# Rotary embedding in float32 on one core: 1 MB of x loaded first, larger end pieces, and five tiles instead of four added on TensorE

## The chip, the cores and the metric

The kernel runs on one core of a Trainium2 chip. Times are device microseconds (us) of one execution. A kernel is run several times; one run of the kernel before took 231.49 us instead of 164.6. It counts as slow and enters no ratio. A ratio here is the mean time of one kernel's fast runs over the mean of the other's fast runs in the same rounds, so it is not quite the ratio of the medians that are quoted beside it.

## The reference

x has shape (8, 2048, 8, 64): batch, position, head, feature. cos and sin have shape (2048, 32). Everything is float32.

```python
x1, x2 = x[..., :32], x[..., 32:]
out1 = x1 * cos - x2 * sin
out2 = x1 * sin + x2 * cos
return np.concatenate([out1, out2], axis=-1)
```

About 33.5 MB are read and 33.5 MB written, so the question is how close the kernel comes to keeping the DMA engines full.

## The kernel before

x is cut into 16 slabs of 2 MB (128 partitions x 4096 columns, 16 KB a partition). Nine slab buffers (`xt`) are used in turn. A slab is worked on in two units of 2048 columns, and its result is written over x in the same buffer. A unit is of one of three kinds:

```python
    kinds = {}
    for i in (5, 10):
        kinds |= {(i, 0): "C", (i, UNIT): "B"}
    # A: GpSimd t2 = x_swapped*(-sin, sin); VectorE t1 = x*cos; VectorE xt = t1 + t2
    # B: GpSimd t2, VectorE t1 as in A; TensorE adds them (eye @ t1 + eye @ t2 in PSUM);
    #    ScalarE copies the sum from PSUM to xt, 512 columns at a time
    # C: VectorE t1 = x*cos and t2 = x*sin, no GpSimd; TensorE adds with eye and -eye; ScalarE copies
```

So B takes one VectorE pass away, and C takes GpSimd's two multiplies away; both give ScalarE four copies. The loads are issued by SyncE, the stores by ScalarE:

```python
    def cuts(i):                      # loads of slab i, in columns
        if i == 0:
            return [HD, HD, 2 * HD, UNIT]     # HD = 512, UNIT = 2048
        return [SLAB]                          # 4096
    def pieces(i):                    # units of work of slab i
        if i == 0:
            return [HD, HD, 2 * HD, UNIT]
        if i == last:
            return [UNIT, 2 * HD, HD, HD]
        return [UNIT, UNIT]
    # ... load(0) issues sin after its first cut; cos is loaded on ScalarE's queue
    LAG = 2
    for i in range(last + 1):
        if i == last:
            for k in range(i - LAG, i):
                store(k, 0, SLAB)
        for lo, n in spans(pieces(i)):
            rotate(i, lo, n)                   # B and C put copies on ScalarE here
            if i == last:
                store(i, lo, n)
        if LAG <= i < last:
            store(i - LAG, 0, SLAB)            # issued by ScalarE, behind those copies
        if i > LAG and i - LAG - 1 + NBUF <= last:
            load(i - LAG - 1 + NBUF)           # needs the store of slab i - 3
```

The copies and the stores are kept in program order on ScalarE. When slab 5 has copies, the stores of slabs 3 and 4 stand behind all eight of them.

## Time and profile before

| | before |
|---|---|
| time, median | 164.64 us (runs: 164.57, 164.64, 231.49) |
| span of the profiled run | 163.0 us |
| DMA | 67.66 MB, mean 415 GB/s, both queues together 98% of sixteen engines' span |
| VectorE, GpSimd busy | 143.4 us (88%), 139.4 us (86%) |

From the page of the kernel before: the busy tenths of VectorE, GpSimd and the DMA engines in 40 slices of 4.1 us, and the two DMA queues (q1 has the loads that SyncE issues, q10 the stores and cos that ScalarE issues).

```profile
DVE  0587999999999999999899999999999999999900
POOL 1599999999999999799999999956999999995000
DMA  4999999999999999999999999999999999999995
...
q1 hardware_dynamic: 2880, 33.82, 49.5%
q10 hardware_dynamic: 2880, 33.82, 48.7%
```

The DMA line has no slice below 9 between the first and the last. VectorE and GpSimd are nearly as full, but they finish 8 and 12 us before the span does. So the bytes bound this kernel, and the other engines matter where they leave the DMA engines without work.

The Trainium skill, page "DMA: Bandwidth & Descriptors", section "Specifications", gives a fabric ceiling of 435 GB/s. The trace agrees: 431 GB/s on average between 30 and 150 us, and 424 to 439 in its stretches of 10 us (the views count a packet whole where it starts, so a stretch can come out a little above the ceiling).

The next lines are from the timeline of the kernel before. Columns: start, duration, engine, line, operation, output and inputs, count; in brackets the idle time before it and what ended it. They show where VectorE starts slab 10's C unit and when ScalarE is done with that slab's copies.

```profile
100.21 2.28 DVE L144 TENSOR_TENSOR t<-xt,cos_ps 128x2048 f32<-128x2048 f32 x1
...
119.32 0.59 ACT L158 COPY xt<-o 128x512 f32<-128x512 f32 x1 [1.13 <-PE o L157]
119.38 3.26 ACTq L183 DMA_DIRECT2D out_dram<-xt  x4
```

Between the C unit's start and the batch of stores lie 19.2 us (19.3 us for slab 5: 55.53 to 74.83). In that time no store is issued, though slabs 8 and 9 are finished, and the DMA engines live on loads. Such a stretch is called a hold below: hold 1 belongs to the first slab with a C unit, hold 2 to the second. The individual DMA packets in the trace show how close the loads came to running out. This table was worked out from those packets, not printed by the profile; "first packet" is when the first of the sixteen engines starts on it, "landed" is when the first and the last engine is done.

```
kernel before            issued   first packet   landed (first, last engine)
load  of slab 11          52.15      72.99         77.79 - 79.25   last load queued in hold 1
store of slab 3           74.83      77.80         82.68 - 83.91   first held store
load  of slab 15         109.91     116.75        121.60 - 123.43  last load of all
store of slab 8          119.38     121.61        126.47 - 127.68  first held store
```

Each time the held stores arrived shortly before the loads ended.

### The profile page before, as it was taken

To read this page: it belongs to the slowest core of one execution; us is meant where nothing else is said; L and a number is where in the kernel's file an instruction comes from. 1 tells how busy PE (TensorE), PEld (TensorE's weight loads), DVE (VectorE), ACT (ScalarE), POOL (GpSimd) and SP (SyncE) were. 2 spreads that over 40 slices of the span, in tenths; PEclk is the share of its full clock that TensorE was granted. 3 is DMA by queue.
4 is the path that set the end of the run, shared out by engine and by line. 5 is a ranking of instruction groups with operands and counts; after the bars stand their busy time and mean duration, and the time that the engine had idled before them with its cause. 6 is when DMAs were issued, how large, how long until landed. Compare 5 with 4: busy or idle time off the path is not lost. (4 is left out here: it accounts for less than half of the span.)

```text
span 163.0 us, 480 instructions
## 1 busy us (share of the span) xinstructions
PE 33.3 (20%) x64; PEld 13.4 (8%) x64; DVE 143.4 (88%) x71; ACT 12.0 (7%) x20; POOL 139.4 (86%) x74
## 2 busy tenths in 40 slices
PE   0000000000000079993000000899920000000000
PEld 0000000000000024440000000244400000000000
DVE  0587999999999999999899999999999999999900
ACT  3300000000000002232000000022410000000000
POOL 1599999999999999799999999956999999995000
PEclk9999999999999999999555555579997555555555
DMA  4999999999999999999999999999999999999995
GB/s 137 383 432 442 406 398 426 438 438 418 438 434 426 430 434 430 426 434 438 422 428 438 424 422 446 430 414 446 434 422 430 442 422 422 446 426 430 434 402 207
DMA packets 5763, 67.66 MB, mean 415 GB/s; under 512 B 640, under 2 KB 640, under 8 KB 1664
## 3 DMA queue, kind: packets, MB, share of 16 engines
q1 hardware_dynamic: 2880, 33.82, 49.5%
q10 hardware_dynamic: 2880, 33.82, 48.7%
q14 instruction: 3, 0.02, 0.0%
HBM read 34.08 MB, written 33.55 MB: 415 GB/s over the span
## 5 line engine op out<-in xcount | busy, mean ns | idle before, releaser
L138 POOL TENSOR_TENSOR t<-xt,sin_sb 128x1024 f32<-128x1024 f32 (+2 forms) x34 | 70.7, 2081 | 10.8 <-DVE xt L151 6.3
L144 DVE TENSOR_TENSOR t<-xt,cos_ps 128x2048 f32<-128x2048 f32 (+2 forms) x36 | 73.9, 2056 | 1.0
L138 POOL TENSOR_TENSOR t<-xt,nsin 128x1024 f32<-128x1024 f32 (+2 forms) x34 | 70.8, 2082 | 0.0
L151 DVE TENSOR_TENSOR xt<-t,t 128x2048 f32<-128x2048 f32 (+2 forms) x32 | 64.8, 2025 | 5.6 <-POOL t L138 2.1
L172 PE MATMUL o<-t,eye 128*128 128x512 f32 x16 | 11.3, 800 | 85.8 <-DVE t L144 85.8
L176 ACT COPY xt<-o 128x512 f32<-128x512 f32 x8 | 4.7, 586 | 94.5 <-DVE t L144 55.3
L172 PEld LDWEIGHTS o<-t,eye 128*128 128x128 f32 x16 | 3.9, 256 | 90.6 <-issue 90.6
L156 PE MATMUL o<-t,eye 128*128 128x512 f32 x16 | 8.2, 592 | 0.0
L157 PE MATMUL o<-t,eye 128*128 128x512 f32 x16 | 8.2, 592 | 0.0
L173 PE MATMUL o<-t,neye 128*128 128x512 f32 x8 | 6.2, 862 | 0.2 <-DVE t L161 0.2
L158 ACT COPY xt<-o 128x512 f32<-128x512 f32 x8 | 4.7, 586 | 9.0 <-PE o L157 9.0
L108 DVE COPY cos_ps<-cos_sb 128x512 f32<-128x512 f32 x1 | 0.7, 694 | 5.0 <-DMA cos_sb<-in_cos_dram 5.0
L161 DVE TENSOR_TENSOR t<-xt,sin_ps 128x2048 f32<-128x2048 f32 x2 | 4.6, 2281 | 0.0
L173 PE MATMUL o<-t,eye 128*128 128x512 f32 x8 | 4.1, 592 | 0.0
L157 PEld LDWEIGHTS o<-t,eye 128*128 128x128 f32 x16 | 3.0, 190 | 3.8 <-issue 3.8
L156 PEld LDWEIGHTS o<-t,eye 128*128 128x128 f32 x16 | 3.0, 190 | 3.8 <-issue 3.8
L173 PEld LDWEIGHTS o<-t,neye 128*128 128x128 f32 x8 | 2.0, 278 | 4.9 <-issue 3.3
L173 PEld LDWEIGHTS o<-t,eye 128*128 128x128 f32 x8 | 1.5, 190 | 1.9 <-issue 1.9
L106 ACT ACT_TABLE_LOAD x1 | 1.3, 1283 | 1.2 <-PEq L215 1.2
L106 ACT ACTIVATE nsin<-sin_sb 128x512 f32<-128x512 f32 x1 | 0.6, 630 | 3.2 <-DMA sin_sb<-in_sin_dram 3.2
L109 ACT COPY sin_ps<-sin_sb 128x512 f32<-128x512 f32 x1 | 0.6, 579 | 0.0
L96 POOL MEMSET eye<- 128x128 f32 x1 | 0.2, 205 | 0.3 <-POOLq L215 0.3
(6 smaller groups left out, 1.0 us busy)
## 6 DMA issues: line engine op xcount, KB each, us to landing
xt<-in_x_dram SPq DMA_DIRECT2D x15, 2048.0 KB, 27.6
out_dram<-xt ACTq DMA_DIRECT2D x15, 2048.0 KB, 15.3
xt<-in_x_dram SPq DMA_DIRECT2D x1, 1024.0 KB, 7.8
out_dram<-xt ACTq DMA_DIRECT2D x1, 1024.0 KB, 10.3
xt<-in_x_dram SPq DMA_DIRECT2D x2, 256.0 KB, 4.3
xt<-in_x_dram SPq DMA_DIRECT2D x1, 512.0 KB, 5.8
out_dram<-xt ACTq DMA_DIRECT2D x1, 512.0 KB, 8.9
out_dram<-xt ACTq DMA_DIRECT2D x2, 256.0 KB, 7.6
```

What stands on the lines that cost most here:

```text
L106: nc.scalar.mul(nsin, sin_sb, -1.0)
L108: nc.vector.tensor_copy(cos_ps, cos_sb)
L138: nc.gpsimd.tensor_mul(out=t2u[:, :, u, :].rearrange("p (r h) d -> p r h d", h=H), in0=xu[:, :, 1 - u, :].rearrange("p (r h) d -> p r h d" ...
L144: nc.vector.tensor_mul(out=t1.rearrange("p (r k d) -> p r k d", r=nr, d=Dh), in0=xk, in1=rep(cos_ps[:, r0 : r0 + nr, :], 2 * H),)
L151: keep(nc.vector.tensor_add(out=xt, in0=t1, in1=t2))
L156: nc.tensor.matmul(o, eye, t1[:, cs], start=True, stop=False)
L157: nc.tensor.matmul(o, eye, t2[:, cs], start=False, stop=True)
L158: keep(nc.scalar.copy(xt[:, cs], o))
L161: nc.vector.tensor_mul(out=t2.rearrange("p (r k d) -> p r k d", r=nr, d=Dh), in0=xk, in1=rep(sin_ps[:, r0 : r0 + nr, :], 2 * H),)
L172: nc.tensor.matmul(o, eye, t1u[:, gs, u, :], start=True, stop=False)
L173: nc.tensor.matmul(o, eye if u else neye, t2u[:, gs, 1 - u, :], start=False, stop=True)
L176: keep(nc.scalar.copy(xu[:, gs, u, :], o.rearrange("p (g d) -> p g d", d=Dh)))
```

## The change

The intent: start with one large transfer, avoid small pieces at both ends, and give TensorE one more addition, so that VectorE has one pass less. The tiles also move from slabs 5 and 10 to slabs 4, 8 and 11. (The new tile on slab 8 is a B: two of the five, the C units, do without GpSimd, as before.)

```diff
     def cuts(i):
-        if i == 0:
-            return [HD, HD, 2 * HD, UNIT]
-        return [SLAB]
+        return [UNIT, UNIT] if i == 0 else [SLAB]
 
     def pieces(i):
         if i == 0:
-            return [HD, HD, 2 * HD, UNIT]
+            return [2 * HD, 2 * HD, UNIT]
         if i == last:
-            return [UNIT, 2 * HD, HD, HD]
+            return [UNIT, 2 * HD, 2 * HD]
         return [UNIT, UNIT]
...
     kinds = {}
-    for i in (5, 10):
+    for i in (4, 11):
         kinds |= {(i, 0): "C", (i, UNIT): "B"}
+    kinds[(8, 0)] = "B"
```

## The prediction

> **What bounds the kernel now.** The DMA engines. The page's DMA line shows 9 tenths or more in every slice but the first and last; the two queues fill 49.5% and 48.7% of sixteen engines' span. In the trace's packets 16 KB take 611 ns, so one 2 MB slab costs 8 x 0.611 = 4.89 us of all engines, and there are 32 slab moves. From 3.0 to 160.5 us the engines never pause. VectorE (88%) and GpSimd (86%) matter only where they let the DMA queues run dry.
>
> **Where that nearly happens.** ScalarE issues the stores in program order, behind its PSUM copies. (The Trainium skill, "DMA: Bandwidth & Descriptors", section "Anatomy of one DMA": the engines wait on no semaphore; the issuing sequencer does. The trace agrees: finished slabs 3 and 4 are not stored until 74.83 us, with slab 5's last copy.) In the timeline the first held batch leaves 19.3 us after the first C multiply starts (55.53 to 74.83), the second 19.2 us after (100.21 to 119.38). Meanwhile DMA lives on loads, limited by nine buffers. Loads ran out only at about 78.5 us (first store packet 77.80) and 122.4 us (121.61): 1 to 2 us to spare.
>
> **What the change does.**
> - Head: sin queues behind 1 MB of x, not 256 KB. 8 KB packets (309 ns) replace pairs of 159 and 84 ns: about 0.15 us, and up to 0.5 us of ramp. GpSimd starts near 7.3 instead of 5.74 us, and runs both sin multiplies first, so slab 0 ends on VectorE at about 19.3 instead of 17.82 us.
> - Tail: 0.07 us of packets. VectorE ends at 155, DMA at 162: off the path.
> - TensorE: slab 8 loses one VectorE add (2.3 us). VectorE ends near 153, which buys nothing: stores are queued there.
> - Slabs 4, 8, 11 instead of 5, 10. This is what counts.
>   - First hold: C starts at 19.3 + 3 x 9.42 = 47.6; batch leaves at 66.9, packets at about 68.6. DMA has 11 loads and 2 stores, two moves (9.8 us) fewer: dry at about 68.5. Idle 0 to 1 us.
>   - Slab 8: copies hold stores 6 to 8 to about 94 us; four stores and four loads are queued till about 98. No idle.
>   - Second hold: C starts at 47.6 + 6.9 + 6 x 9.42 - 2.3 = 108.7 at most; batch leaves at about 127.6, packets at 129.3. DMA has 16 loads and 9 stores, one move more: dry at 122.4 + 4.9 = 127.3 at most. Idle about 2 us.
>
> **Sum.** The end hangs on the second release: 129.3 instead of 122.4 us, with one store (4.9 us) fewer behind it and 0.1 us of tail: +1.9 us. 164.64 + 1.9 gives **166.5 us**, range 164.3 to 168.2. Chances: faster by over 2%: 2%; within 2%: 86%; slower by over 2%: 12%.
>
> **Right or wrong.** DMA share dips at 66 to 70 us (slightly) and clearly at 126 to 130 us; stores 9 to 11 leave together near 127.6. VectorE finishes near 153 while the span grows. First GpSimd multiply near 7.3 us.
>
> **What would make it wrong.** A faster start or a higher TensorE clock that releases the stores by 125 us: then no dip, and 0.3 to 0.8 us of small packets are gained (about 164). A cold TensorE in slabs 8 or 11, or slab 8's hold draining the queues: 168 or more.

## The result

The changed kernel takes 167.32 us at the median (166.95 to 167.41, four runs), the kernel before 164.63. The ratio is 1.016, 95% interval 1.014 to 1.018: slower, by less than 2%, inside the predicted range.

The same lines of the page of the changed kernel:

```profile
DVE  0349999999999999999998999999999999999100
POOL 1299999999999979999999999999799999970000
DMA  5999999999999999999999999999997999999995
...
q10 hardware_dynamic: 2736, 33.82, 48.8%
q1 hardware_dynamic: 2592, 33.82, 48.7%
```

VectorE's busy time fell from 143.4 to 140.3 us and the span still grew from 163.0 to 165.6 us. There is one new thing in the DMA line: a 7 three quarters of the way along. The windows view of that stretch, 1 us a row (start and end, length, busy time and instructions of TensorE, its weight loads, VectorE, ScalarE, GpSimd, then the TensorE clock, the DMA share and GB/s), shows what it is:

```profile
126.00:127.00 1.00, 1.00 (x3) 0.38 (x2) 1.00 (x1) 0.57 (x1) 1.00 (x1) 1.00 1.07 459
127.00:128.00 1.00, 1.00 (x3) 0.19 (x1) 0.80 (x2) 0.02 (x1) 1.00 (x2) 1.00 0.36 148
128.00:129.00 1.00, 0.11 (x1) 0.00 (x0) 1.00 (x1) 0.59 (x1) 1.00 (x1) 1.00 0.00 0
129.00:130.00 1.00, 0.00 (x0) 0.00 (x0) 0.97 (x2) 0.00 (x0) 1.00 (x2) 1.00 1.25 524
```

In the row from 128 to 129 us no packet starts, while VectorE and GpSimd are busy nearly throughout. (A packet is counted where it starts, so single rows can pass the ceiling, and 0 does not mean that nothing moves: by the single packets the engines fall idle one after another between 127.3 and 128.4 us, and all sixteen are idle from 128.43 to 129.06.) For comparison, the corresponding stretch of the kernel before, around its own second batch of stores:

```profile
119.00:120.00 1.00, 0.28 (x1) 0.00 (x0) 1.00 (x1) 0.59 (x1) 1.00 (x1) 1.00 1.07 459
120.00:121.00 1.00, 0.00 (x0) 0.00 (x0) 0.97 (x2) 0.00 (x0) 1.00 (x2) 1.00 0.88 377
121.00:122.00 1.00, 0.00 (x0) 0.00 (x0) 1.00 (x1) 0.00 (x0) 1.00 (x1) 1.00 1.08 459
122.00:123.00 1.00, 0.00 (x0) 0.00 (x0) 1.00 (x1) 0.00 (x0) 1.00 (x1) 1.00 1.00 426
```

The timeline of the changed kernel, with slab 11's C unit and ScalarE's last copy of that slab:

```profile
108.86 2.27 DVE L143 TENSOR_TENSOR t<-xt,cos_ps 128x2048 f32<-128x2048 f32 x1
...
128.15 0.59 ACT L157 COPY xt<-o 128x512 f32<-128x512 f32 x1 [1.13 <-PE o L156]
128.21 3.12 ACTq L182 DMA_DIRECT2D out_dram<-xt  x4
```

The C unit starts 8.65 us later than before (108.86 against 100.21), and the batch leaves 8.83 us later (128.21 against 119.38). The packets of the changed kernel, in the same table as above:

```
changed kernel           issued   first packet   landed (first, last engine)
load  of slab 10          44.88      63.00         67.79 - 68.60   last load queued in hold 1
store of slab 2           66.98      67.83         72.94 - 73.75   first held store
load  of slab 15         109.64     117.66        127.09 - 128.29  last load of all
store of slab 8           96.25     117.83        126.95 - 128.42  last store before hold 2
store of slab 9          128.21     129.06        134.01 - 134.17  first held store
```

The DMA engines had one slab more of other work by then (4.9 us), but the batch leaves 8.8 us later. The 3.9 us between exceed the 2.3 us to spare at this place (mid-landing near 122.5, less 119.38 and 0.85). Summed over the sixteen engines, the pause between 127.25 and 129.25 us is worth 1.4 us.

The lines of the start, first for the kernel before, then for the changed one: GpSimd's first multiply and the first store.

```profile
5.74 0.72 POOL L138 TENSOR_TENSOR t<-xt,sin_sb 128x256 f32<-128x256 f32 x1 [4.44 <-DMA sin_sb<-in_sin_dram]
...
17.85 0.35 ACTq L183 DMA_DIRECT2D out_dram<-xt  x1
```

```profile
7.42 1.26 POOL L137 TENSOR_TENSOR t<-xt,sin_sb 128x512 f32<-128x512 f32 x1 [6.11 <-DMA sin_sb<-in_sin_dram]
...
19.71 0.35 ACTq L182 DMA_DIRECT2D out_dram<-xt  x1
```

The second bracket says what GpSimd waited for: sin, now queued behind 1 MB of x. VectorE starts its steady work 1.9 us later.

The pause is not the whole difference. The span is 2.6 us longer, and the packets add up as follows (per engine, worked out from the trace): the time the packets themselves took rose by 1.5 us (160.0 to 161.5) although their sizes alone would have saved 0.2; the time between first and last packet with no packet rose by 0.9 us (the pause less a faster start); and the wait from the last packet to the end rose by 0.2 us. So in this sum of one profile longer packets are as large an entry as the pause. They are not a second loss of that size: of the 1.7 us, 0.46 lies behind the pause; what came before it kept the queues busy longer and so shortened the pause (see the last point but one on the prediction).

### The profile page after: what moved, and what is told of

Its sections match the earlier page's. It is cut to its first block, busy times and chain, and to the rows that moved or that the text cites. A ratio compares the mean times of both kernels' runs of the same rounds, so it can differ in the third digit from the quotient of the medians.

```text
span 165.6 us, 498 instructions
## 1 busy us (share of the span) xinstructions
PE 42.4 (26%) x80; PEld 17.1 (10%) x80; DVE 140.3 (85%) x66; ACT 14.3 (9%) x24; POOL 138.9 (84%) x70
## 4 chain that ended last, share of the span: by engine, by line
DVE 57%; DMA 22%; PE 6%; issue 4%; POOL 2%; ACTq 1%; DVEq 0%; SPq 0%; ACT 0%; POOLq 0%
DVE t L143 30%; DVE xt L150 25%; DMA out_dram<-xt 19%; DMA sin_sb<-in_sin_dram 4%; PE o L155 3%; PE o L156 3%; POOL t L137 2%; DVE t L160 1%; ACTq L182 1%; DVEq L150 0%; SPq L82 0%; ACT xt L157 0%; POOLq L137 0%
## 5 line engine op out<-in xcount | busy, mean ns | idle before, releaser
L137 POOL TENSOR_TENSOR t<-xt,sin_sb 128x1024 f32<-128x1024 f32 (+1 forms) x32 | 70.7, 2209 | 8.6 <-DMA sin_sb<-in_sin_dram 6.1
L143 DVE TENSOR_TENSOR t<-xt,cos_ps 128x2048 f32<-128x2048 f32 (+1 forms) x34 | 73.4, 2167 | 0.9
L137 POOL TENSOR_TENSOR t<-xt,nsin 128x1024 f32<-128x1024 f32 (+1 forms) x32 | 70.7, 2211 | 0.0
L150 DVE TENSOR_TENSOR xt<-t,t 128x2048 f32<-128x2048 f32 (+1 forms) x29 | 62.2, 2144 | 5.7 <-POOL t L137 2.3
L171 PE MATMUL o<-t,eye 128*128 128x512 f32 x16 | 11.3, 797 | 67.3 <-DVE t L143 67.3
L155 PE MATMUL o<-t,eye 128*128 128x512 f32 x24 | 13.6, 649 | 18.2 <-DVE t L143 18.2
L156 PE MATMUL o<-t,eye 128*128 128x512 f32 x24 | 13.1, 631 | 0.0
L171 PEld LDWEIGHTS o<-t,eye 128*128 128x128 f32 x16 | 3.9, 257 | 72.1 <-issue 72.1
L175 ACT COPY xt<-o 128x512 f32<-128x512 f32 x8 | 4.7, 586 | 74.3 <-PE o L172 74.3
L157 ACT COPY xt<-o 128x512 f32<-128x512 f32 x12 | 7.0, 586 | 34.1 <-DMA xt<-in_x_dram 21.4
L155 PEld LDWEIGHTS o<-t,eye 128*128 128x128 f32 x24 | 5.0, 212 | 24.9 <-issue 24.9
L156 PEld LDWEIGHTS o<-t,eye 128*128 128x128 f32 x24 | 4.9, 202 | 6.4 <-issue 6.4
L172 PE MATMUL o<-t,eye 128*128 128x512 f32 x8 | 4.1, 592 | 0.0
L172 PEld LDWEIGHTS o<-t,eye 128*128 128x128 f32 x8 | 1.5, 190 | 1.9 <-issue 1.9
```

Of the source, the lines that this page charges most:

```text
L137: nc.gpsimd.tensor_mul(out=t2u[:, :, u, :].rearrange("p (r h) d -> p r h d", h=H), in0=xu[:, :, 1 - u, :].rearrange("p (r h) d -> p r h d" ...
L143: nc.vector.tensor_mul(out=t1.rearrange("p (r k d) -> p r k d", r=nr, d=Dh), in0=xk, in1=rep(cos_ps[:, r0 : r0 + nr, :], 2 * H),)
L150: keep(nc.vector.tensor_add(out=xt, in0=t1, in1=t2))
L155: nc.tensor.matmul(o, eye, t1[:, cs], start=True, stop=False)
L156: nc.tensor.matmul(o, eye, t2[:, cs], start=False, stop=True)
L157: keep(nc.scalar.copy(xt[:, cs], o))
```

## The experiments

Theory H (the hold): stores of finished slabs stand behind ScalarE's copies of a C/B slab; the changed slab numbers and the later start make that hold outlast the work queued for the DMA engines. Rival E: the new ends (first load, end pieces) carry the loss. Rival P: five tiles on TensorE cost by themselves. Later a theory S was added: packets that take longer when one queue joins the other. All experiments gave correct results. Ratios are against the kernel before in the same rounds, with the 95% interval.

### e1: the second pair on slab 10 instead of 11

```diff
-    for i in (4, 11):
+    for i in (4, 10):
```

> The changed kernel with its second C/B pair on slab 10 instead of 11; nothing else differs. Theory H (the hold): stores 9 to 11 were issued at 128.2 us because they stand behind slab 11's copies, 0.9 us after the DMA queues ran dry; on slab 10 the copies come 9.4 us sooner, the batch leaves near 119 us with loads still queued, so the pause of the DMA engines near 128 us vanishes: 165.2 to 166.0 us, 1.4 us or more under the changed kernel's 167.3. Rival E (the new ends cost it: a later start, larger last pieces): no difference, 167.3. Rival P (five tiles on TensorE cost by themselves): no difference, 167.3.

Measured: 166.11 us (165.52 to 166.86), ratio 1.0091 [1.0055, 1.0126]. The batch leaves at 118.26 us, and the windows view has no gap (nor, by the packets, has the stretch around this batch, 118 to 126 us):

```profile
126.00:127.00 1.00, 0.00 (x0) 0.00 (x0) 0.97 (x1) 0.00 (x0) 1.00 (x2) 0.50 1.11 475
127.00:128.00 1.00, 0.00 (x0) 0.00 (x0) 0.83 (x1) 0.00 (x0) 1.00 (x1) 0.50 0.92 393
128.00:129.00 1.00, 0.00 (x0) 0.00 (x0) 1.00 (x1) 0.00 (x0) 1.00 (x1) 0.50 1.04 442
```

One slab number, with the same tiles and the same ends, takes the pause away and about 1.2 us. E and P, which expected no difference, miss this as causes of the whole loss. But the kernel stays 0.9% above the one before, a little above what H expected: the profile has 1.7 us of packet time beyond what the sizes of the packets need more than the kernel before.

### e2: without the tile on slab 8

```diff
-    kinds[(8, 0)] = "B"
```

> The changed kernel without the added tile of slab 8, so TensorE does less and VectorE one add (2.3 us) more. Theory H: the add delays slab 11 by 2.3 us, so the held batch leaves near 130.5 us while the DMA queues still run dry near 127.4: a pause of some 3.5 us, 169 to 170 us, slower than the changed kernel. Rival P: less on TensorE, so 167 or faster. Rival E: no difference, 167.3.

Measured: 168.63 us (168.0 to 169.41), ratio 1.0244 [1.020, 1.0287]: slower than the changed kernel with less work on TensorE, against rival P. The batch leaves at 129.04 us, and the pause is longer, 2.6 us per engine instead of 1.4 by the packets:

```profile
127.00:128.00 1.00, 1.00 (x4) 0.46 (x3) 1.00 (x1) 0.59 (x1) 1.00 (x1) 1.00 0.21 82
128.00:129.00 1.00, 0.94 (x3) 0.11 (x1) 1.00 (x1) 0.03 (x1) 1.00 (x1) 1.00 0.00 0
129.00:130.00 1.00, 0.00 (x0) 0.00 (x0) 0.80 (x2) 0.56 (x1) 1.00 (x2) 1.00 0.54 229
```

The batch moved by 0.8 us, not by the 2.3 us expected, so the time fell just short of the expected 169: the C unit did start 1.9 us later (110.73 us), but the hold behind it was 18.3 us instead of 19.4. So the added tile helps in the changed kernel, by releasing the stores sooner as far as this trace shows.

### e3: only the new ends; e4: only the new tiles

e3 is the changed kernel with the slabs (5, 10) and no slab 8; e4 is the kernel before with the slabs 4, 8 and 11.

> Only the ends of the change: 1 MB of x leads, no small pieces; TensorE has slabs 5 and 10 as in the kernel before. Theory H: VectorE starts 1.9 us later, the second batch leaves near 121.3 us against queues that run dry near 122, so at most 0.3 us of pause, and the first ramp is 0.4 us shorter: 164.2 to 165.0. Rival E: the ends carry the loss, 166.5 to 167.5. Rival P: 164.6, as before.

> Only the tiles of the change: slabs 4, 8 and 11, with the kernel before's small pieces at both ends. Theory H: VectorE starts 1.9 us sooner than in the changed kernel, so the second batch leaves near 126.4 us, just before the queues run dry near 127.7: no pause or under 0.3 us, 164.9 to 165.8; the two halves of the change do not add up, since the loss needs both. Rival E: 164.6. Rival P: the tiles carry the loss, 167.

Measured: e3 165.54 us (164.97 to 166.12), ratio 1.0042 [1.0013, 1.0072]; e4 165.34 us (164.84 to 165.56), ratio 1.0037 [1.0016, 1.0058]. Together the halves make 0.8%; both at once cost 1.6%. That is what H needs: in e4 the batch leaves at 126.29 us and only a short dip is left (0.35 us per engine), because VectorE starts sooner.

```profile
125.00:126.00 1.00, 1.00 (x3) 0.19 (x1) 0.80 (x2) 0.09 (x1) 1.00 (x2) 1.00 0.92 393
126.00:127.00 1.00, 0.19 (x1) 0.00 (x0) 1.00 (x1) 0.59 (x1) 1.00 (x1) 1.00 0.59 246
127.00:128.00 1.00, 0.00 (x0) 0.00 (x0) 0.97 (x2) 0.00 (x0) 1.00 (x2) 1.00 1.25 524
```

e4 fell where H put it. e3 missed: 0.5 us above the expected range with no pause at all. The ends cost something of their own.

### e5: the stores ahead of the copies

The changed kernel, complete, but slab 9's and 10's stores are issued before slab 11's copies. Nothing waits less than it must: the stores still wait for VectorE's last add of their slab.

```diff
+    done = set()
     for i in range(last + 1):
...
+        if i == 11:
+            for k in range(i - LAG, i):
+                store(k, 0, SLAB)
+                done.add(k)
         for lo, n in spans(pieces(i)):
             rotate(i, lo, n)
...
-        if LAG <= i < last:
+        if LAG <= i < last and i - LAG not in done:
             store(i - LAG, 0, SLAB)
```

> The changed kernel, all three slabs and both ends as they are, but ScalarE issues the stores of slabs 9 and 10 ahead of slab 11's copies instead of behind them. Theory H: these stores then leave when VectorE ends the slabs, near 100 and 109 us, and queue behind stores 6 to 8; the pause of the DMA engines near 128 us is gone though TensorE's work and VectorE's times stay as they were: 165.2 to 166.3 us, like the run with slab 10. Rivals E and P: 167.3.

Measured: 164.9 us (164.71 to 165.77), ratio 1.0028 [1.0005, 1.005]. The two stores now leave at 99.10 and 108.54 us, and the stretch of the pause is full:

```profile
126.00:127.00 1.00, 1.00 (x3) 0.19 (x1) 0.80 (x2) 0.05 (x1) 1.00 (x2) 1.00 1.05 442
127.00:128.00 1.00, 0.14 (x1) 0.00 (x0) 1.00 (x1) 0.59 (x1) 1.00 (x1) 1.00 1.03 442
128.00:129.00 1.00, 0.00 (x0) 0.00 (x0) 1.00 (x1) 0.00 (x0) 1.00 (x1) 1.00 0.92 393
```

With all five tiles, both new ends and the same copies at nearly the same times (the last 0.4 us sooner), a change of order on ScalarE brings back 1.3 of the 1.6%. This is the strongest test of H: e5's slowest run is 1.2 us below the changed kernel's fastest. And it went further than expected: the packets' own time fell from 161.5 to 160.1 us per engine too. Of these 1.4 us, 0.44 lies behind the place of the pause. In the changed kernel the stores of whole slabs after the pause took 616 to 623 ns a 16 KB packet at the mean of each slab, in e5 in the same place 611 to 612; the pause seems to have a price beyond its length, though the profile does not show by what. But 0.76 us lies between 60 and 90 us, ahead of the changed order, where both programs are the same. That part is not the edit's doing, and how much it adds to e5's gain is not shown.

### e6: the same order in the kernel before

The same edit, ahead of the copies of slabs 5 and 10.

> The kernel before, with the stores of the two finished slabs issued ahead of the copies of slabs 5 and 10. Theory H: the kernel before had no pause to lose, so nothing to gain by it: within 0.3 us of 164.6. Theory S (a second loss beside the pause: packets take longer when the other queue joins in, as in the stretches near 21, 78 and 121 us of the first four runs): with stores always queued there are fewer joinings after the first, so 164.0 to 164.6.

Measured: 164.62 us (164.38 to 164.63), ratio 0.9997 [0.9986, 1.0009]. No gain, as H expected where there was no pause. (Theory S, with 164.0 to 164.6, is hardly told from H by this run.) It is the version to prefer all the same: it is no slower, and its order should not hang on which slabs have copies, though it was run with slabs 5 and 10 alone. That no version beat the kernel before fits the DMA line: it leaves only the start and the end.

### e7, e8: head and tail apart

e7 is the kernel before with only the new `cuts(0)` and `pieces(0)`; e8 with only the new `pieces(last)`.

> The kernel before with only the head of the change: 1 MB of x in one load ahead of sin, first pieces of 1024 columns. The run with both new ends was 0.9 us above the kernel before without any pause; its packets took 1.1 us longer than the sizes need, most of it around the first store and the first held batch. If the head brings that (theory S, by moving when the queues meet): 165.0 to 165.6. If it is the tail: 164.2 to 164.5, the gain of the ramp alone.

> The kernel before with only the tail of the change: the last slab's second half as two pieces of 1024 columns instead of 1024, 512 and 512. In all runs with the new tail the span ends 1.35 to 1.6 us after the last packet instead of 1.17. If that is the tail's: 164.7 to 164.9, and nothing else moves. If the tail brings the whole 0.9 us of the run with both ends: 165.3 to 165.6.

Measured: e7 165.33 us (164.86 to 165.56), ratio 1.0043 [1.0029, 1.0058]; e8 164.73 us (164.62 to 164.97), ratio 1.001 [0.9998, 1.0022]. The ends' own cost is the head's. The tail is not told apart from nothing, though its span did end 1.43 us after the last packet instead of 1.17. (That wait is not the new tail's alone: e9 below, with the old tail, has 1.35, and e12 with the new one 1.22.)

### e9, e10: the head's loads and pieces apart

e9 has only the new `cuts(0)` (one load of 1 MB ahead of sin), e10 only the new `pieces(0)`.

> The new head alone cost 0.8 us at the median without any pause of the DMA engines. This is the kernel before with only its loads changed (1 MB of x in one load ahead of sin); the pieces that VectorE and GpSimd work on stay small. If the loads carry the head's loss (their order and size set when the two queues meet and how their packets interleave): 165.0 to 165.5. If the larger first pieces do: 164.2 to 164.6.

> The reverse: the kernel before with only the first pieces enlarged to 1024 columns and the loads as they were. If the larger pieces carry the head's loss: 165.0 to 165.5. If the loads do: 164.4 to 164.8, as before.

Measured: e9 165.45 us (164.71 to 166.49), ratio 1.0055 [1.0025, 1.0086]; e10 164.84 us (164.67 to 165.08), ratio 1.0013 [1.0000, 1.0026], a hair above its range. So the loads seem to carry the head's cost, though the two intervals just touch. e9's runs also spread over 1.8 us, those of the kernel before in the same rounds over 0.7; each of e9's six is slower than the one before it, so a drift is not excluded. The profiled run of e9 was its fastest (164.71), so no profile shows what the slow ones lose.

### e11: no tile on TensorE

```diff
-    for i in (4, 11):
+    for i in ():
         kinds |= {(i, 0): "C", (i, UNIT): "B"}
-    kinds[(8, 0)] = "B"
```

> The changed kernel with no tile on TensorE, so every sum is on VectorE and every product by sin on GpSimd. Theory H: ScalarE has no copies, so no store is ever held and the DMA engines do not pause in the middle; but VectorE has three adds (7 us) more and ends near 161 us instead of 153.7, so the last pieces are stored late and the DMA engines run thin at the end: 166 to 167.5. Rival P: without TensorE's work it is faster than the changed kernel by more than the pause, 165 or less.

Measured: 167.11 us (166.96 to 167.45), ratio 1.0151 [1.0137, 1.0165], as H expected and against P. Without copies nothing is held, but VectorE now ends at 161.5 us and the DMA engines run dry twice near the end:

```profile
150.00:152.00 2.00, 1.97 (x2) 0.00 (x0) 1.66 (x3) 1.00 0.33 139
...
160.00:162.00 2.00, 1.39 (x2) 0.00 (x0) 0.00 (x0) 1.00 0.59 242
```

(No TensorE columns here: it has no instruction.) The same total as the changed kernel, by the opposite fault. TensorE's tiles are needed; it is their place among the stores that has to be right.

### e12: both repairs

The changed kernel with e5's order and with slab 0's loads cut as before.

> The changed kernel with two repairs: slab 9's and 10's stores issued ahead of slab 11's copies, and slab 0's loads back in the kernel before's small cuts with sin second. All five tiles on TensorE, the larger pieces for VectorE and the new tail stay. If the held stores and the new loads are the whole loss, 164.4 to 164.9, level with the kernel before. If something else in the change costs (five tiles, the larger pieces), 165.2 or more.

Measured: 165.29 us (164.92 to 166.09), ratio 1.0038 [1.0016, 1.006]. This missed. Putting the loads back gained nothing on top of e5 (1.0028; the intervals overlap). Its six runs fall into two groups, 164.9 and 165.6 to 166.1; the profiled one, 165.64, has no pause common to all engines, but its last store lands 1.7 us apart on the first and the last engine, against 1.1 us in the kernel before. So the remaining 0.3 to 0.4% is not the loads alone. By what was expected of this run, a small cost of the five tiles or of the larger pieces stays possible; Rival P is refuted as the cause of the 1.6%, not of this rest.

## Why the prediction was right

Point by point, with what the runs showed.

- DMA bounds the kernel, and VectorE's saved pass buys nothing at the end: right. VectorE ended at 153.7 us (predicted near 153) instead of 155.0, and the span grew. (At the second hold the pass does count, as the prediction's -2.3 has it: without it e2 is slower.)
- The later start: right. GpSimd began at 7.42 us (7.3 predicted), and slab 0 was done at 19.71 us (19.3).
- First hold, idle 0 to 1 us: right at the lower end. The batch left at 66.98 us (66.9 predicted) and its first packet started 0.85 us later, where the prediction had allowed 1.7. The loads ended at 67.8 to 68.6 us, so there was no pause, and the slight dip at 66 to 70 us that the prediction named as a sign did not come.
- Slab 8: right. Stores 6 to 8 left from 94.38 us (94 predicted), with work queued throughout.
- Second hold: right in mechanism and nearly in size. C at 108.86 us (108.7), batch at 128.21 (127.6), first packet at 129.06 (129.3), queues dry at 127.1 to 128.4 (127.3). The pause was worth 1.4 us instead of "about 2". That the first packet agrees so well is partly luck: the batch left 0.6 us later than predicted and its first packet took 0.85 us instead of 1.7, and the two errors nearly cancel. e1, e2, e4 and e5 move or remove the pause and the time follows.
- The sum was short: +1.9 us predicted, +2.7 measured. The term that is missing is the length of the packets. The prediction counted 611 ns for every 16 KB packet; in the changed kernel's profile the stores took 624 ns and the loads 619 ns at the mean, against 611 and 616 before, which makes 1.85 us per engine over the 120 packets of each queue. With that term added to a pause of 1.4 us and the shorter start taken off, the sum is about right. But in the prediction's own terms the end hangs on the second release, and that came 0.2 us sooner than predicted. What is missing therefore lies behind it: there the packets took 0.46 us longer than the commonest duration of their size (0.01 in the kernel before), and the wait after the last packet rose by 0.2. The longer packets ahead of the release, some 1.3 us more than before, went into the pause: the engines ran dry at 127.7 us on average, not at 127.3. This is a reading of one profile; no run separates the two parts.
- One branch would have been wrong: that without a pause the larger first packets would be a gain (about 164 us). The ramp is 0.4 us shorter in the packets, but the new head alone was 0.4% slower (e7), it seems by its loads (e9).

What stays open. Why the new loads make the packets longer and the times spread, and what makes up the last 0.3 to 0.4% in e5 and e12. The trace shows where packets are long: in every kernel around the first store, when the second queue joins the first (in the kernel before 33 load packets between 19.1 and 21.8 us, up to 1226 ns instead of 611), and in several kernels with the new loads again when the held stores of hold 1 start: between 60 and 90 us, 0.5 to 0.9 us per engine beyond the commonest duration in the changed kernel, e1, e2, e3 and e9, but 0.15 to 0.21 in e5 and e7, and at most 0.19 in every kernel with the old loads. Since e5 has the changed kernel's program up to slab 10, this part differs between executions or chips of the same code. Behind the pause it is 0.46, 0.43 and 0.39 us in the changed kernel, e2 and e4, the three with a pause or dip in hold 2, and at most 0.14 in all others. Theory S, that these meetings are the cause, was not tested apart from the loads, and e12 speaks against the loads being the whole of it.

## What to carry to other kernels

On a kernel bound by DMA, ask of each engine that issues transfers what stands ahead of them in its program order: finished results behind another tile's copies are the same as results not finished, and the queues live on what was issued before. Add up that reserve (here 4.9 us a slab) against the length of the hold (here 19 us) whenever slabs, buffers or the start move; a margin of 2 us is spent by a change that looks harmless. Better, issue the stores that are ready ahead of the copies: it cost nothing where there was no pause (e6) and removed the pause where there was one (e5).

## What the Trainium skill lacked or had wrong

- "DMA: Bandwidth & Descriptors", section "Specifications", gives an HBM limit of about 358 GB/s for a core with no condition beside it. The condition stands only further down: the section "Measured (HBM→SBUF, 128 partitions, SWDGE, issued from GpSimd)" says that each core gets about 358 GB/s when both cores of a pair stream. With this one core active the kernel before held 424 to 439 GB/s over stretches of 10 us (415 over the whole span), near the fabric ceiling of 435.
- Section "Specifications" of that page gives a first-byte latency of about 0.6 us for transfers issued by SyncE and ScalarE. From the start of the issue to the first packet the runs show 0.85 us on empty queues (128.21 to 129.06) and 2.2 to 4.5 us when the other queue had loads waiting (3.9 us for the first store of the kernel before, 17.85 to 21.76). The page has no figure for the second case, and a hold is costed with it.
- The same page, section "Anatomy of one DMA", says that the DMA engines wait on no semaphore and the issuing sequencer does. The section describes DMAs issued by GpSimd; in the runs the stores that ScalarE issues fit it (slab 3's leaves at 74.83 us, with slab 5's last copy). What no page spells out is the consequence: stores in program order behind copies of another tile, 19.2 to 19.3 us long.
- No page says that packets of one queue grow longer when the other queue starts: 33 packets of up to 1226 ns instead of 611 around the first store in the kernel before, some 0.5 us per engine. Nor does one say that runs of one such kernel may differ by 1.8 us (e9). That the one explains the other, and the cause of either, is not shown here.
